# Reordering the front of the expert stage in a two-layer hybrid decoder trunk

## The chip, the cores and the metric

One core of one Trainium2 chip runs the whole kernel. The metric is the device time of one execution in microseconds; three runs of the kernel before are known, and one more execution was profiled.

## The reference, cut to what matters

256 tokens of width 1024 pass two layers. Each layer normalises the tokens with an adaLN modulation (six vectors from `silu(c) @ ada_w`), projects them once, runs three token mixers side by side (retention, a spatial-gating MLP, a sparse attention with three branches), projects back and adds. Then follows a grouped mixture of experts:

```
h2 = rms_norm(x, norm_ffn_g[l]) * (1.0 + sc2) + sh2
probs = softmax(h2 @ router_w); best group of 4, then the top 2 experts in it
for e in range(16):
    a = silu(h2 @ w_gate[e]) * (h2 @ w_up[e])
    out = out + (gates[..., e:e+1] * a) @ w_down[e]
x = x + g2 * out
```

All arrays are float32. The weights of one expert are 4 MB (`w1`, gate and up) and 2 MB (`wd`, down), so the 16 experts of one layer are 96 MB (of 1024 x 1024 bytes), two thirds of what a layer reads.

## The kernel before, in words

The kernel is written with a tile framework. Program order gives each instruction its priority, and a scheduler at build time makes one fixed list for each engine from it: an instruction that is ready by the scheduler's own estimate may go ahead of an earlier one that is not. `tc.issue_after(ins)` forces what is written inside it behind `ins` on the same engine. Buffers are classes with a fixed number: `ring` has 11 slots of 1 MB for all large weights, `wh` 5 buffers of 0.5 MB (the split halves of weights in attention, two quarters of `wd` in the expert stage), `c6` 2 buffers of 1 MB (attention probabilities; the other half of `wd`), `f4` 3 buffers of 0.5 MB (attention operands; the experts' outputs `yy`), `t2` 7 smaller ones. PSUM has 4 banks "W" and 4 banks "D". A DMA on SyncE's queue waits for its buffer, and all behind it wait too.

A layer's attention part splits float32 weights into a rounded part `hi` and a remainder `lo` and multiplies three times (`mm3`). `ORDER[l]` is the order of the loads: `s0` to `s5` are parts of the input projection, `o0` and `o1` the output projection, `a..` the adaLN weights. `S4P` says how many of the eight steps of projection `s4` (retention's gate and the MLP's gate) are written at each of eight places among the four attention heads; what is left comes behind the heads. In the first layer that is all of them, in the second one. `FILL` spreads the adaLN tasks (`ada_half`: two VectorE instructions of 128x1024, L195) over places; two of them stand behind each of the first four experts.

The expert stage (`moe`) computes router and gates on VectorE, ranks tokens per expert with small matmuls (`prank`), and builds the one-hot matrix `Pm` (L1225). `tokens` scales the transposed tokens `xs` by the norm (L887), rounds them to `hi` (L888) on ScalarE and takes `lo = xs - hi` on GpSimd (L890) or VectorE (L892). `gather` multiplies `hi` and `lo` by `Pm` into four PSUM banks and writes `xg`, half by ScalarE (L992), half by VectorE (L990). `group(0)` gathers four fixed experts of full width; then `sort` orders the other twelve by their counts (its result `idI` is read by SyncE's register loads, L1257, to address their weights, and `rkP` by the later gathers). For each expert: one-hot and its transposes (`tables_`, L1025 to L1040), the up-projection into `pgu` (L1049, or L1058 for the experts of small width), activation (L1064), the previous expert's down-projection `py` (L1082) and scatter `mo`. For every expert but a group's first, `LEAD` = 2 of the 8 chunks are multiplied ahead of the tables. `extras` and `overflow` serve experts with more tokens than their width.

Of the kernel before, what the change touches and what calls it, by code (L numbers as in the profile page):

```python
# [23 lines left out]
LEAD = 2  # L24
# [13 lines left out]
F2 = False  # L38
# [7 lines left out]
S4P = ("00000000", "01111111")  # L46
WP = (3, 3)
TASKV = ((2, 3, 4, 5), (2, 3, 4, 5))
XRA = ((1, 1), (1, 0))
# [14 lines left out]
ORDER = ["s3 cmp s5 a01.0 a01.1 a01.2 a01.3 s4 a02.0 a02.1 o1 o0 a02.2 a02.3 a10.0 a10.1 a10.2 a10.3".split(),  # L64
# [778 lines left out]
def moe(tc, nc, l, env):  # L843
# [19 lines left out]
    if True:  # L863
# [18 lines left out]
        def tokens():  # L882
            for q in range(2):
                for tt in range(2):
                    d = slice(512 * q, 512 * q + 512)
                    xs = pts[2 * q + tt]
                    A.activation(xs, xs, AF.Copy, scale=rt[:, tt:tt + 1])  # L887
                    A.copy(hi[:, tt, d], xs)  # L888
                    if XRA[q][tt]:
                        G.tensor_tensor(lo[:, tt, d], xs, hi[:, tt, d].bitcast(F32), op=OP.subtract)  # L890
                    else:
                        late.append(lambda tt=tt, d=d, xs=xs: V.tensor_tensor(lo[:, tt, d], xs, hi[:, tt, d].bitcast(F32), op=OP.subtract))  # L892
# [82 lines left out]
        def gather(Pm, n, xg_):  # L975
            per = 2
            for c0 in range(0, 8, per):
                pg = bank("W", "pgx")
                for u in range(per):
                    k = 0  # L980
                    for tt in range(2):
                        for src in (hi, lo):
                            T.matmul(pg[:, n * u:n * u + n], src[:, tt, P * (c0 + u):P * (c0 + u) + P], Pm[:, tt, :],
                                     start=k == 0, stop=k == 3)
                            k += 1
                for u in range(per):
                    c = c0 + u
                    xg, c_ = xg_(c0, u)
                    if u % 2:
# [224 lines left out]
        def group(g, rank_of):  # L1214
# [8 lines left out]
            for tt in range(2):  # L1223
                for p, o, w, k in runs:
                    V.tensor_tensor(Pm[:, tt, o:o + w * k].rearrange("p (e s) -> p e s", e=k), iot[:, 0:1, 0:w].to_broadcast([P, k, w]),  # L1225
                                    rank_of(tt, p, k).unsqueeze(2).to_broadcast([P, k, w]), op=OP.is_equal)
            xg = []
            while late:
                late.pop(0)()
# [5 lines left out]
            gather(Pm, n, piece)  # L1235
# [7 lines left out]
        last = [None, None, None]  # L1243
        xgs = group(0, lambda tt, p, k: rk[:, tt, ST0 + p:ST0 + p + k])
        rkP, gP, inP, idI, rkx = sort()
        pend, seen, done = None, -1, []
        for g4, members in enumerate(XGR):
            order = members
            for k, (p, xo_, w) in enumerate(order):
# [3 lines left out]
                if p != "x":  # L1253
# [9 lines left out]
                    for i in range(2):  # L1263
                        wb.append(tl("wh", [1024], "wd_"))
                        Y.dma_start(wb[i], sd[:, 1024 * i:1024 * i + 1024])
                    w2_ = tl("c6", [2, 1024], "wd2")
                    Y.dma_start(w2_, sd[:, 2048:4096].rearrange("p (f n) -> p f n", f=2))
                    wb += [w2_[:, 0], w2_[:, 1]]
# [9 lines left out]
                CA = LEAD if k else 0  # L1278
# [10 lines left out]
                if p != "x":  # L1289
                    with fence_(rk_, F2):  # L1290
                        g_["fill"](FILL[l][6][seen])
                if seen == 0:
                    ovf = extras()
# [91 lines left out]
```

## Time and profile before

| | |
|---|---|
| three runs | 864.17, 871.84, 871.11 us; median 871.11 |
| the profiled execution | 865.73 us, of it span 864.1 us |
| TensorE matmul | 762.8 us busy (88%) |
| TensorE weight load | 481.0 us (56%) |
| VectorE | 461.3 us (53%) |
| ScalarE | 278.8 us (32%) |
| GpSimd | 74.7 us (9%) |
| DMA | 292.95 MB, mean 339 GB/s |
| first layer's expert stage | from about 217 to 452 us |
| second layer's expert stage | from about 626 us to the end |

Busy shares are averages over stages with different limits: attention is bound by VectorE and TensorE while loads run ahead, the expert stage by the weights. Matmuls are pipelined, so a busy TensorE is not one at its peak.

### The profile page before, as it was taken

Reading aid. Unit: us, or ns where it says so; the run is one execution under the profiler, and the core shown is the slowest. Engines: PE = TensorE matmul, PEld = TensorE weight load, DVE = VectorE, ACT = ScalarE, POOL = GpSimd, SP = SyncE. Lnnn points to the kernel's source line nnn. Section 1 sums busy time; section 2 is a strip of 40 time slices with the busy share of each in tenths; the row PEclk is TensorE's granted clock in tenths of the full one; section 3 lists DMA queues with packets and bytes.
Section 4 is the critical chain, followed back from the end, with each engine's and each line's share of the span. In section 5 each row is a group of like instructions: output and inputs, shape, how many; then the busy total and the mean of one; then the engine's idle time right before and its main releaser. Section 6 shows DMA issues by size and latency. Waiting matters only on the chain. (4 is left out here: it accounts for less than half of the span.)

```text
span 864.1 us, 14353 instructions
## 1 busy us (share of the span) xinstructions
PE 762.8 (88%) x5460; PEld 481.0 (56%) x5460; DVE 461.3 (53%) x1183; ACT 278.8 (32%) x663; POOL 74.7 (9%) x89
## 2 busy tenths in 40 slices
PE   4789999885899999897988998999789999988795
PEld 3677736784446455343347786678544645534342
DVE  6997869997623223122136898998652322322123
ACT  6246566624111112011026644675411111111010
POOL 2232010211000000000001231011100000000000
PEclk9899869988899999899897998999989999999798
DMA  8959829878779999999999579468838999999995
GB/s 355 420 212 367 334 94 361 293 289 328 279 276 410 418 418 418 417 421 414 420 419 375 178 260 419 149 226 319 300 111 320 421 418 411 419 420 418 414 418 201
DMA packets 46881, 292.95 MB, mean 339 GB/s; under 512 B 5456, under 2 KB 6224, under 8 KB 15952
## 3 DMA queue, kind: packets, MB, share of 16 engines
q1 hardware_dynamic: 45360, 289.76, 84.3%
q10 hardware_dynamic: 1440, 2.16, 0.8%
q8 instruction: 46, 0.75, 0.3%
q14 instruction: 35, 0.29, 0.1%
HBM read 290.84 MB, written 1.05 MB: 338 GB/s over the span
## 5 line engine op out<-in xcount | busy, mean ns | idle before, releaser
L1049 PE MATMUL pgu<-w1slot,xg 128*64 128x512 f32 x640 | 172.5, 627 | 18.3 <-DMA w1slot<-w_dram 13.2
L1049 PEld LDWEIGHTS pgu<-w1slot,xg 128*64 128x64 f32 x640 | 54.9, 141 | 100.4 <-issue 98.8
L195 DVE SCALAR_TENSOR_TENSOR adaslot<-adaslot,sb__90 128x1024 f32<-128x1024 f32 x72 | 92.1, 1290 | 0.0
L1091 DVE SCALAR_TENSOR_TENSOR yy<-py,gc,yy 64x512 fp32r<-64x512 f32 x40 | 30.0, 750 | 112.3 <-ACT yy L1090 112.3
L352 PE MATMUL pz<-hhi,whl 128*128 128x256 f32 x256 | 72.5, 294 | 10.1 <-ACT hhi L423 10.1
L1090 ACT ACTIVATE yy<-py,gc 64x512 fp32r<-64x512 f32 x40 | 27.4, 684 | 165.7 <-PE py L1082 149.5
L353 PE MATMUL pz<-hlo,whl 128*128 128x256 f32 x256 | 74.5, 294 | 0.9 <-DVE hlo L424 0.9
L354 PE MATMUL pz<-hhi,whl 128*128 128x256 f32 x256 | 74.2, 295 | 0.4 <-DVE whl L348 0.2
L348 POOL TENSOR_TENSOR whl<-winslot,whl 128x512 fp32r<-128x512 f32 (+1 forms) x24 | 34.6, 1441 | 388.7 <-ACT whl L346 303.2
L1058 PE MATMUL pgu<-w1slot,xg 128*32 128x256 f32 x896 | 59.6, 387 | 4.0 <-DMA w1slot<-w_dram 4.0
L352 PEld LDWEIGHTS pz<-hhi,whl 128*128 128x128 f32 x256 | 49.2, 197 | 14.1 <-ACT hhi L423 12.9
L1038 DVE CAST pgT<-ppg 128x256 fp32r<-128x256 f32 x34 | 14.4, 424 | 78.2 <-PE ppg L1036 78.2
L1065 DVE TENSOR_TENSOR a<-a,pgu 128x256 f32<-128x256 f32 (+1 forms) x34 | 12.4, 366 | 76.5 <-ACT a L1064 76.3
L353 PEld LDWEIGHTS pz<-hlo,whl 128*128 128x128 f32 x256 | 50.7, 198 | 3.0 <-DVE hlo L424 1.7
L354 PEld LDWEIGHTS pz<-hhi,whl 128*128 128x128 f32 x256 | 50.5, 199 | 2.1 <-DVE whl L348 1.0
L346 ACT CAST whl<-winslot 128x512 fp32r<-128x512 f32 (+1 forms) x72 | 40.5, 578 | 26.2 <-PE pz L354 24.4
L1058 PEld LDWEIGHTS pgu<-w1slot,xg 128*32 128x32 f32 x896 | 28.7, 110 | 33.0 <-issue 16.9
L1064 ACT ACTIVATE a<-pgu 128x256 f32<-128x256 f32 (+1 forms) x34 | 11.6, 341 | 108.4 <-PE pgu L1049 91.7
L348 DVE TENSOR_TENSOR whl<-winslot,whl 128x512 fp32r<-128x512 f32 (+1 forms) x48 | 34.5, 725 | 10.2 <-ACT whl L346 10.0
L1099 ACT ACTIVATE yy<-py,gc 128x256 fp32r<-128x256 f32 x14 | 6.6, 474 | 102.6 <-PE py L1107 102.6
L354 PE MATMUL pw<-yhi,whl 128*128 128x256 f32 x128 | 36.4, 290 | 3.5 <-DVE whl L348 3.5
L1082 PE MATMUL py<-wd,aT 128*64 128x512 f32 x160 | 38.9, 592 | 0.0
(500 smaller groups left out, 1504.7 us busy)
## 6 DMA issues: line engine op xcount, KB each, us to landing
w1slot<-w_dram SPq DMA_DIRECT2D x128, 1024.0 KB, 17.2
adaslot<-adaw_dram SPq DMA_DIRECT2D x40, 1024.0 KB, 6.6
wd<-wd_dram SPq DMA_DIRECT2D x32, 1024.0 KB, 15.1
winslot<-win_dram SPq DMA_DIRECT2D x14, 1024.0 KB, 15.9
slot<-adaw_dram SPq DMA_DIRECT2D x8, 1024.0 KB, 18.9
woslot<-wout_dram SPq DMA_DIRECT2D x8, 1024.0 KB, 11.0
slot<-win_dram SPq DMA_DIRECT2D x6, 1024.0 KB, 18.0
cmpslot<-cmpw_dram SPq DMA_DIRECT2D x4, 1024.0 KB, 13.7
```

The lines of the kernel that those rows point to most:

```text
L195: V.scalar_tensor_tensor(wb, wb, 1.0, sb_, op0=OP.mult, op1=OP.mult, accum_out=mv_[:, b:b + 1])
L346: A.copy(hi, wv)
L348: (G if wc[0] % WP[fl[0]] == 0 else V).tensor_tensor(lo, wv, hi.bitcast(F32), op=OP.subtract)
L352: T.matmul(o, a[0], b[0], start=start, stop=False, skip_group_check=True)
L353: T.matmul(o, a[0], b[1], start=False, stop=False, skip_group_check=True)
L354: T.matmul(o, a[1], b[0], start=False, stop=stop, skip_group_check=True)
L1038: V.tensor_copy(pT, pp_[:, :S])
L1049: lastu[0] = T.matmul(gu[64 * j:64 * j + 64, :], xg(c)[:, xs:xs + CAP], w1(c, j), start=c == 0, stop=c == 7, skip_group_check=True).ins
L1058: lastu[0] = T.matmul(gu[SW * t:SW * t + SW, 0:256], xg(c)[:, xs:xs + SW], wv, start=c == 0, stop=c == 7, skip_group_check=True).ins
L1082: T.matmul(py[64 * hf:64 * hf + 64, :], aT[:, ib, 64 * j:64 * j + 64], wd(fc)[:, 512 * hf:512 * hf + 512], start=fc == 0, stop=fc == 3, sk ...
L1090: ya = A.activation(y[0:64, :], py[r_, :], AF.Copy, scale=gc[r_, :])
L1091: V.scalar_tensor_tensor(y[64:128, :], py[r_, :], gc[r_, :], y[0:64, :].bitcast(F32), op0=OP.mult, op1=OP.subtract)
```

## The change

- `tokens` makes `hi` in one ScalarE instruction from the unscaled `xs`, and all four `lo` in one VectorE instruction each, written behind `Pm`; GpSimd has no part in it.
- `gather` for the first group multiplies all `hi` into four banks, then all `lo`.
- `sort` is written behind the first expert's up-projection and activation, ahead of `extras`; the first expert too multiplies two chunks ahead of its tables.
- The two ada tasks behind the first expert are forced behind `Pm`.
- In the first layer `s4` is loaded behind `a01.0` instead of behind `a01.3`, and seven of its steps stand among the heads.
- The first expert's `wd` is loaded in four pieces, three into `f4` buffers and one into `wh`.

```
-S4P = ("00000000", "01111111")
+S4P = ("01111111", "01111111")
...
-ORDER = ["s3 cmp s5 a01.0 a01.1 a01.2 a01.3 s4 a02.0 a02.1 o1 o0 ...
+ORDER = ["s3 cmp s5 a01.0 s4 a01.1 a01.2 a01.3 a02.0 a02.1 o1 o0 ...
...
-                    A.activation(xs, xs, AF.Copy, scale=rt[:, tt:tt + 1])
-                    A.copy(hi[:, tt, d], xs)
-                    if XRA[q][tt]:
-                        G.tensor_tensor(lo[:, tt, d], xs, hi[:, tt, d].bitcast(F32), op=OP.subtract)
-                    else:
-                        late.append(lambda tt=tt, d=d, xs=xs: V.tensor_tensor(lo[:, tt, d], xs, hi[:, tt, d].bitcast(F32), op=OP.subtract))
+                    A.activation(hi[:, tt, d], xs, AF.Copy, scale=rt[:, tt:tt + 1])
+                    late.append(lambda tt=tt, d=d, xs=xs: V.scalar_tensor_tensor(
+                        lo[:, tt, d], xs, rt[:, tt:tt + 1], hi[:, tt, d].bitcast(F32), op0=OP.mult, op1=OP.subtract))
...
-        def gather(Pm, n, xg_):
+        def gather(Pm, n, xg_, ahead=False):
             per = 2
+            pgs = {}
+
+            def products(c0, srcs):
+                if c0 not in pgs:
+                    pgs[c0] = bank("W", "pgx")
+                for u in range(per):
+                    for src in srcs:
+                        for tt in range(2):
+                            T.matmul(pgs[c0][:, n * u:n * u + n], src[:, tt, P * (c0 + u):P * (c0 + u) + P], Pm[:, tt, :],
+                                     start=src is hi and tt == 0 and u == 0, stop=src is lo and tt == 1, skip_group_check=True)
+            if ahead:
+                for c0 in range(0, 8, per):
+                    products(c0, (hi,))
             for c0 in range(0, 8, per):
...
+                products(c0, (lo,) if ahead else (hi, lo))
...
             xg = []
-            while late:
-                late.pop(0)()
+            with tc.issue_after(pm0[0].ins):
+                while late:
+                    late.pop(0)()
...
-            gather(Pm, n, piece)
+            gather(Pm, n, piece, g == 0)
...
-        rkP, gP, inP, idI, rkx = sort()
...
-                    for i in range(2):
-                        wb.append(tl("wh", [1024], "wd_"))
+                    for i in range(2 if seen else 4):
+                        wb.append(tl("wh" if seen or i == 3 else "f4", [1024], "wd_"))
                         Y.dma_start(wb[i], sd[:, 1024 * i:1024 * i + 1024])
-                    w2_ = tl("c6", [2, 1024], "wd2")
...
+                    if seen:
+                        w2_ = tl("c6", [2, 1024], "wd2")
...
-                CA = LEAD if k else 0
+                CA = LEAD if k or not g4 else 0
...
-                    with fence_(rk_, F2):
+                    with fence_(pm0[0], seen == 0):
                         g_["fill"](FILL[l][6][seen])
                 if seen == 0:
+                    rkP, gP, inP, idI, rkx = sort()
                     ovf = extras()
```

(`F2` was False; `pm0[0]` is the last instruction that builds `Pm`.)

## Rows read from the trace of the kernel before

**Rows 1.** Stretch windows of five stages: busy us, instructions, granted clock, DMA share, GB/s.

```profile
184.00:200.00 16.00, 13.24 (x90) 12.26 (x89) 12.20 (x24) 2.68 (x7) 1.41 (x1) 0.79 0.69 241
...
224.00:248.00 24.00, 22.23 (x94) 8.19 (x96) 9.38 (x44) 2.50 (x4) 0.00 (x0) 0.93 0.46 161
248.00:430.00 182.00, 166.49 (x1300) 84.83 (x1298) 42.19 (x123) 23.42 (x46) 0.00 (x0) 0.95 1.01 417
...
624.00:641.00 17.00, 11.35 (x59) 7.78 (x60) 14.05 (x72) 3.54 (x5) 0.05 (x1) 0.80 0.03 10
...
672.00:848.00 176.00, 163.41 (x1317) 83.26 (x1320) 41.48 (x121) 23.20 (x46) 0.00 (x0) 0.96 1.01 417
```

**Rows 2.** Timeline of SyncE's queue, first layer: start, duration, DMA issues merged.

```profile
198.11 0.33 SPq L1265 DMA_DIRECT2D wd__2228<-wd_dram  x1
...
242.03 0.33 SPq L1265 DMA_DIRECT2D wd__2378<-wd_dram  x1
...
258.41 2.11 SPq L105 DMA_DIRECT2D w1slot<-w_dram  x4
```

**Rows 3.** The same, second layer.

```profile
614.30 0.42 SPq L1265 DMA_DIRECT2D wd__6994<-wd_dram  x1
640.22 5.11 SPq L105 DMA_DIRECT2D w1slot<-w_dram  x4
...
663.62 0.35 SPq L105 DMA_DIRECT2D w1slot<-w_dram  x1
```

**Rows 4.** Waits of SyncE's queue from 605 to 665 us: total, times, longest.

```profile
SPq L1257 <- DVE tmq L1011: 18.5, 1, 18.5
```

**Rows 5.** Timeline of VectorE, first layer, residual update to first expert.

```profile
201.70 1.22 DVE L195 SCALAR_TENSOR_TENSOR adaslot<-adaslot,sb__90 128x1024 f32<-128x1024 f32 x1
...
202.85 0.87 DVE L811 SCALAR_TENSOR_TENSOR xT<-pw,mod,xT 128x256 f32<-128x256 f32 x2
...
207.90 1.21 DVE L195 SCALAR_TENSOR_TENSOR adaslot<-adaslot,sb__90 128x1024 f32<-128x1024 f32 x1
...
211.89 1.17 DVE L926 TENSOR_SCALAR wn<-wn 128x32 f32<-128x32 f32 x1
...
213.06 1.24 DVE L915 TENSOR_TENSOR W<-gsc 128x6 f32<-128x6 f32 x1
214.22 0.15 DVE L916 TENSOR_TENSOR W<-gsc 128x6 f32<-128x6 f32 x1
...
216.92 0.75 DVE L1225 TENSOR_TENSOR Pm<-iot,rk 128x256 fp32r<-128x256 f32 x2
...
218.15 0.68 DVE L892 TENSOR_TENSOR lo<-xs,hi 128x512 fp32r<-128x512 f32 x1
...
225.35 0.47 DVE L1025 TENSOR_SCALAR Pd<-iot,rk 128x128 f32<-128x128 f32 x2
```

**Rows 6.** Timeline of GpSimd, first layer.

```profile
211.76 3.74 POOL L890 TENSOR_TENSOR lo<-xs,hi 128x512 fp32r<-128x512 f32 x3 [6.20 <-ACT hi L888]
```

**Rows 7.** Timeline of TensorE, gather to first up-projection, both layers.

```profile
217.48 0.55 PE L983 MATMUL pgx<-Pm,hi 128*128 128x256 f32 x1 [0.96 <-DVE Pm L1225]
...
225.77 0.30 PE L1034 MATMUL ppg<-ident,Pd 128*128 128x128 f32 x1 [2.99 <-DVE Pd L1025]
...
227.99 10.05 PE L1049 MATMUL pgu<-w1slot,xg 128*64 128x512 f32 x38
...
635.47 0.43 PE L1034 MATMUL ppg<-ident,Pd 128*128 128x128 f32 x2 [3.86 <-DVE Pd L1025]
...
636.17 10.50 PE L1049 MATMUL pgu<-w1slot,xg 128*64 128x512 f32 x40
```

**Rows 8.** Stretch windows of VectorE alone, first layer's heads and behind.

```profile
104.00:128.00 24.00, 14.99 (x49) 0.64 0.35 131
128.00:192.00 64.00, 61.78 (x133) 0.95 0.85 312
```

More of the change, by code (lines that the diff above doesn't have):

```diff
@@ L37 @@
 F1 = True
-F2 = False
 ENG3 = (mybir.EngineType.PE, mybir.EngineType.Activation, mybir.EngineType.DVE, mybir.EngineType.Pool)
@@ L45 @@
 NPA = ("0011", "0011")
-S4P = ("00000000", "01111111")
+S4P = ("01111111", "01111111")
 WP = (3, 3)
 TASKV = ((2, 3, 4, 5), (2, 3, 4, 5))
-XRA = ((1, 1), (1, 0))
 XSV = ((1, 1), (1, 0))
@@ L62 @@
 C3 = TWO_PI - C1 - C2
-ORDER = ["s3 cmp s5 a01.0 a01.1 a01.2 a01.3 s4 a02.0 a02.1 o1 o0 a02.2 a02.3 a10.0 a10.1 a10.2 a10.3".split(),
+ORDER = ["s3 cmp s5 a01.0 s4 a01.1 a01.2 a01.3 a02.0 a02.1 o1 o0 a02.2 a02.3 a10.0 a10.1 a10.2 a10.3".split(),
          "s0 s1 s2 cmp s3 a11.0 a11.1 s5 a11.2 a11.3 s4 a12.0 a12.1 o1 o0 a12.2 a12.3".split()]
@@ L973, in gather_few @@
             return xo
-        def gather(Pm, n, xg_):
+        def gather(Pm, n, xg_, ahead=False):
             per = 2
-            for c0 in range(0, 8, per):
[L978 to L985, printed above, removed]
+            pgs = {}
[10 more added lines that the diff above has]
+                    products(c0, (hi,))
+            for c0 in range(0, 8, per):
+                products(c0, (lo,) if ahead else (hi, lo))
                 for u in range(per):
@@ L988, in gather @@
                     xg, c_ = xg_(c0, u)
+                    pg = pgs[c0]
                     if u % 2:
@@ L1224, in group @@
                 for p, o, w, k in runs:
-                    V.tensor_tensor(Pm[:, tt, o:o + w * k].rearrange("p (e s) -> p e s", e=k), iot[:, 0:1, 0:w].to_broadcast([P, k, w]),
+                    pm0[0] = V.tensor_tensor(Pm[:, tt, o:o + w * k].rearrange("p (e s) -> p e s", e=k), iot[:, 0:1, 0:w].to_broadcast([P, k, w]),
                                     rank_of(tt, p, k).unsqueeze(2).to_broadcast([P, k, w]), op=OP.is_equal)
             xg = []
-            while late:
-                late.pop(0)()
+            with tc.issue_after(pm0[0].ins):
+                while late:
+                    late.pop(0)()
             def piece(c0, u):
@@ L1241, in rank_of @@
             return rkP[:, tt, p:p + k]
-        last = [None, None, None]
+        pm0, last = [None], [None, None, None]
         xgs = group(0, lambda tt, p, k: rk[:, tt, ST0 + p:ST0 + p + k])
-        rkP, gP, inP, idI, rkx = sort()
         pend, seen, done = None, -1, []
@@ L1262, in moe @@
                     wb = []
-                    for i in range(2):
-                        wb.append(tl("wh", [1024], "wd_"))
+                    for i in range(2 if seen else 4):
+                        wb.append(tl("wh" if seen or i == 3 else "f4", [1024], "wd_"))
                         Y.dma_start(wb[i], sd[:, 1024 * i:1024 * i + 1024])
-                    w2_ = tl("c6", [2, 1024], "wd2")
-                    Y.dma_start(w2_, sd[:, 2048:4096].rearrange("p (f n) -> p f n", f=2))
-                    wb += [w2_[:, 0], w2_[:, 1]]
+                    if seen:
+                        w2_ = tl("c6", [2, 1024], "wd2")
+                        Y.dma_start(w2_, sd[:, 2048:4096].rearrange("p (f n) -> p f n", f=2))
+                        wb += [w2_[:, 0], w2_[:, 1]]
                 w1 = lambda c, j, wa=wa: wa[c // 2][:, c % 2, j, :]
```

## The prediction

> **What bounds the kernel now.** I read the stretch windows first. In the expert stage of either layer the DMA engines are full (share 1.01, 417 GB/s) while TensorE is busy 166.5 of 182.0 us and 163.4 of 176.0 us [rows 1]: the weights set the pace there, and TensorE has some 15 and 13 us to spare. What is lost lies in front of it. The DMA share is 0.69 from 184 to 200 us, 0.46 from 224 to 248 us and 0.03 from 624 to 641 us [rows 1]: 5.0, 13.0 and 16.5 us without transfers. Since every later byte follows at full rate, a microsecond of restart gained in these gaps is a microsecond off the end, as long as the restart is what the next expert waits for.
>
> Then SyncE's queue, to see why the DMA stood still. In the first layer the second `wd_` piece of the first expert goes out at 198.11, of the third at 242.03; the fifth expert's first weights at 258.41 [rows 2]. In the second layer SyncE sits after 614.72 for 18.5 us on `tmq`, the sort [rows 3, 4], so until 633.2, spends 7.0 us on the twelve register loads, and issues again at 640.22 [rows 3]. But the ring was full anyway: a slot comes free only when TensorE has done two chunks of the first expert, whose run begins at 636.17 [rows 7]. What holds both restarts is the chain from router to first expert.
>
> That chain is read on VectorE, GpSimd and TensorE together [rows 5 to 7]. The gather starts at 217.48; it ends 2.99 us before 225.77, at 222.78; then TensorE waits for `Pd`, which VectorE reaches only at 225.35, behind the sort. In the second layer the same wait is 3.86 us.
>
> **The change part by part.** Times are of the profiled execution, 865.73 us (span 864.1); the median of the three runs is 871.11, 5.4 us above it, the lowest 1.6 below it.
>
> *One-pass halves.* The three `lo` subtractions on GpSimd span 211.76 to 215.50 [rows 6]. In that span three VectorE instructions of the router take 1.17 to 1.24 us, where their neighbour takes 0.15 [rows 5]: about 1.03 us each, 3.1 us a layer on the path, and they go. Added are four `lo` instructions on VectorE behind `Pm`; the one that is there now takes 0.68 [rows 5], so 2.7 us. The sixteen `hi` products cover them: 32 products take 5.30 us (217.48 to 222.78), half of them 2.65 us, and the first `lo` product needs only two of the four. If that cover were gone, up to 2.7 us would return in each layer. ScalarE issues four instead of eight, and is done before `Pm`.
>
> *Hi products first.* The matmuls are as many as before. They hold all four "W" banks at once, so the first expert's bank waits for the first bank's two evictions, at the end of the gather; I add 0.5 us in the first layer, nothing in the second.
>
> *Sort behind the first expert, two chunks ahead of its tables.* The 2.99 and 3.86 us go: the up-projection needs only `xg`, and the tables come between chunks. What is next late is the gather itself. The sort's VectorE work now runs beside an up-projection of 10.05 and 10.50 us [rows 7]. SyncE's register loads need the sort; the fifth expert's weights are its first user, and they are due some 30 us after the up-projection starts (227.99 to 258.41), so this is covered unless the queue puts them earlier (a rival below).
>
> *The fence.* Two ada tasks, four instructions of 1.22 us (4.9 us) [rows 5], move behind `Pm` in the first layer. The list that the scheduler makes put such instructions in front of the residual update at 201.70 and in front of `lg` and `mx` at 206.47 and 207.90, of which the last is shown [rows 5]. Without the last four the update can go about 0.9 us and `mx` about 1.5 us earlier; I count 2.1. Behind `Pm` they can delay evictions by up to one instruction each; and the two ring slots that they hold are freed some 10 us later, for the third expert, whose weights aren't needed for another 20 us.
>
> *First `wd` in f4.* The output buffers are idle from the end of attention. Two `wh` buffers and half of `c6` come free for the next experts: 1.5 MB more before the restart, and no wait at 198.11 and 242.03. One slot of 1.05 MB takes 2.5 us at 417 GB/s [rows 1]. From 242.03 to 258.41 SyncE issued 7.5 such pieces, 18.9 us of transfer, so the fifth expert's first byte moved only at about 262, 3.6 us behind its issue. With the third expert's `wd` already there, and the fourth's weights drawn from 220 on, this backlog is gone by 250. I count 1.5 of the 3.6 us, since TensorE moves less than that and its finished down-projections still release SyncE. In the second layer there is no such backlog, and I count nothing. The first `wd` goes out as four DMAs of 0.5 MB where three went.
>
> The Trainium skill, DMA: Bandwidth & Descriptors, section Bandwidth, speaks against such a split: it asks for at least 1 MiB in one DMA to get 75% of the peak. By it these 2 MB would take a third longer, an estimate of 1.7 us a layer, and the sum below would be 852.9. The rows speak against it: two of seven DMAs of every expert are 0.5 MB already, and the stage runs at 417 GB/s [rows 1].
>
> *s4 between the heads.* The same instructions in another order, in the first layer alone; its two loads pass six ada loads in SyncE's queue, which then come about 5 us later, long before their tasks. VectorE is busy 61.8 of 64 us from 128 to 192 us, so there the order gives nothing; from 104 to 128 it is busy 15.0 of 24 at a granted clock of 0.64 [rows 8]. Bounds: if that stretch ran at the full 2.4 GHz it would take 24 x 0.64 = 15.4 us, 8.6 us less. If s4's 96 matmuls come into it, at the gather's 0.166 us each, 15.9 us, at most half of that is due to a clock at half rate: 8 us more. The trace shows neither. I take nothing, since VectorE's sum is unchanged and it is the full engine right behind, and keep -8.6 and +8.
>
> *The sum.* First layer: 3.1 + 3.0 + 2.1 - 0.5 = 7.7 us on TensorE, and 1.5 us of backlog: 9.2. Second layer: 3.1 + 3.9 = 7.0. Together 16.2 us: 865.7 - 16.2 = 849.5. A median may lie up to 5.4 us higher, as that of the runs before does; I put it in the middle, 852.
>
> **The rivals.**
>
> *A, VectorE becomes the wait.* Behind `Pm` it now has four `lo`, four evictions, `Pd` and in the first layer four ada instructions. If the queue puts the ada work first, the evictions start 4.9 us later there, and what the `lo` products wait for costs another 1 to 2 us in each layer: the gain is 3 and 5.5 us, with the median 860. For it: the scheduler has put ada work in front of `mx` before [rows 5]. Against: the evictions come earlier in the program.
>
> *B, the sort comes too late for SyncE; slower.* In the second layer SyncE already sat on the sort ahead of expert weights [rows 3, 4]. If the sort is queued behind the first expert's activation, some 11 us after the up-projection's start at about 629, its result is there at about 646 (5 us of sort, as an estimate from half of the time between 216.92 and 225.35 [rows 5], where evictions lie between). Then 7.0 us of loads: the DMA restarts at 653. Seven pieces are missing then, 17.6 us, and the fifth expert's first byte moves at 670 instead of 663.62 [rows 3]: 7 us later. In the first layer, with 4.9 us of ada work in front, it would be 265 instead of 262, 3 us later. With the median 881. It decides from a restart later than 646 in the second layer. Against it: VectorE has the sort's inputs at `Pm`, and time for it.
>
> *C, s4 or the fence spoils attention.* 8 us lost before the router in the first layer; the median is 860. If instead the 8.6 us are gained, 843.
>
> *D, nothing.* The scheduler may give the same order again, or the gap may be refilled by another full buffer (`c6` for the fourth expert is released by the second's down-projection, as before): 866 to 871.
>
> **How the numbers follow.** The sum as it stands has 0.56 (its own range 846 to 857, from the two levels of the runs and the 3.6 us of backlog); A 0.16; C 0.12, a third of it on the fast side; B 0.08; D 0.08. The range that leaves out 2 in 10 goes from 843 to 866: 0.1 lies above (B and part of D), and a tenth below, where C's gain and the whole backlog come together. A measurement of this kernel tells about 1% from no change, 8.7 us, so faster means below 862.4: the forecast, C and most of A, 0.8 with some doubt taken off for terms that share one cause, 0.75; within 1% 0.18; slower 0.07.
>
> **What would show it.** On VectorE no router instruction above 0.3 us between `sel` and `rk`, and GpSimd idle there. TensorE going from the last `lo` product into `pgu` without a wait for `Pd`, at about 218 and 629 us if attention keeps its length. The DMA gap of 224 to 248 down to some 6 us, that of the second layer ending at about 631. SyncE's wait on `tmq` gone, or ending before a ring slot is free. From there the expert stages as long as before, at 417 GB/s. The forecast is wrong if ada instructions stand between `Pm` and the first eviction, if SyncE's loads of the sorted indices end after 646, or if the first layer's attention ends more than 3 us earlier or later, as the start of its router shows.

## The result, and the profile after

| | before | changed |
|---|---|---|
| median of five runs, us | 870.88 (862.22 to 871.84) | 846.35 (842.34 to 856.05) |
| ratio | | 0.973, 95% interval 0.966 to 0.980 |

In the runs of the first experiment the ratio was 0.979 (0.974 to 0.985). The forecast was 852, in the range 843 to 866, and faster. Executions more than 1.5% above their kernel's fastest are disturbed ones, which the ratios leave out and the medians and counts of this document do not; the profiled execution of the five runs (856.05, granted clock 0.66 from 520 to 560 us) is one, so the rows of after come from another execution of the same kernel, 848.38 us with a span of 846.8 (0.74 there): 17.4 us below the profiled execution of before.

The stretch windows of the changed kernel, beside [rows 1]:

```profile
184.00:200.00 16.00, 13.61 (x109) 12.77 (x107) 13.69 (x25) 4.10 (x10) 3.58 (x2) 0.89 0.88 310
...
216.00:240.00 24.00, 22.72 (x116) 11.53 (x117) 19.18 (x73) 4.13 (x7) 0.00 (x0) 0.92 0.82 318
240.00:430.00 190.00, 177.45 (x1366) 88.01 (x1366) 45.69 (x129) 26.14 (x50) 0.00 (x0) 0.95 1.01 414
604.00:624.00 20.00, 18.55 (x123) 11.53 (x123) 15.60 (x62) 8.67 (x20) 0.00 (x0) 1.00 0.67 245
655.00:831.00 176.00, 162.88 (x1321) 82.94 (x1324) 41.49 (x121) 23.46 (x46) 0.00 (x0) 0.96 1.01 411
```

The gap of 13.0 us in the first layer is now 24 x (1 - 0.82) = 4.3 us, and the one of 16.5 us in the second is 20 x (1 - 0.67) = 6.6. The expert stages behind them run as before, DMA full, TensorE not.

SyncE's queue, the timeline of the first layer and then of the second (start, duration, issues merged):

```profile
207.33 18.71 SPq L103 DMA_DIRECT2D w1slot<-w_dram  x4
...
226.57 0.56 SPq L1267 DMA_DIRECT2D wd__2376<-wd_dram  x1
...
251.33 1.94 SPq L103 DMA_DIRECT2D w1slot<-w_dram  x4
...
621.55 8.06 SPq L103 DMA_DIRECT2D w1slot<-w_dram  x6
```

And its longest wait from 590 to 650 us (total, times, longest):

```profile
SPq L103 <- PE ppg L1036: 14.1, 1, 14.1
```

The third expert's second `wd_` piece goes out at 226.57 where it went at 242.03 [rows 2]; the fifth expert's first weights at 251.33, not 258.41. In the second layer SyncE issues again at 621.55, not 640.22 [rows 3]; its wait for the sort [rows 4] is gone, and it waits for a free ring slot instead.

VectorE in the first layer, beside [rows 5]:

```profile
209.03 0.19 DVE L893 TENSOR_REDUCE mx<-lg 128x2 f32<-128x32 f32 x1
...
211.89 0.17 DVE L921 TENSOR_SCALAR wn<-wn 128x32 f32<-128x32 f32 x1
...
212.04 0.16 DVE L910 TENSOR_TENSOR W<-gsc 128x6 f32<-128x6 f32 x1
...
213.79 0.75 DVE L1227 TENSOR_TENSOR Pm<-iot,rk 128x256 fp32r<-128x256 f32 x2
214.47 2.73 DVE L886 SCALAR_TENSOR_TENSOR lo<-xs,rt,hi 128x512 fp32r<-128x512 f32 x4
217.12 0.47 DVE L1027 TENSOR_SCALAR Pd<-iot,rk 128x128 f32<-128x128 f32 x2
219.60 0.55 DVE L992 TENSOR_SCALAR xg<-pgx,gs,mod 128x256 f32<-128x256 f32 x1 [2.01 <-ACT xg L994]
...
221.85 1.21 DVE L193 SCALAR_TENSOR_TENSOR adaslot<-adaslot,sb__90 128x1024 f32<-128x1024 f32 x1
...
230.35 0.16 DVE L1017 CAST idI<-inP 128x12 int32<-128x12 f32 x1
```

No router instruction above 0.3 us is left (`wn` 0.17, `W` 0.16, where 1.17 and 1.24 stood), `Pd` is done before the gather ends, and the ada instructions come behind the evictions. That is what the prediction asked to see of VectorE.

TensorE, beside [rows 7]:

```profile
214.36 3.75 PE L980 MATMUL pgx<-Pm,hi 128*128 128x256 f32 x16 [1.01 <-DVE Pm L1227]
217.91 2.85 PE L980 MATMUL pgx<-Pm,lo 128*128 128x256 f32 x16
220.68 1.94 PE L1051 MATMUL pgu<-w1slot,xg 128*64 128x512 f32 x8
...
223.26 12.24 PE L1051 MATMUL pgu<-w1slot,xg 128*64 128x512 f32 x56
...
237.77 1.08 PE L1084 MATMUL py<-wd__2185,aT 128*64 128x512 f32 x4 [0.96 <-issue]
...
614.31 0.17 PE L936 MATMUL prank<-o,ub 128*128 128x16 bf16 x1 [0.44 <-DVE o L924]
...
615.59 2.14 PE L980 MATMUL pgx<-Pm,hi 128*128 128x256 f32 x16 [1.01 <-DVE Pm L1227]
617.57 2.08 PE L980 MATMUL pgx<-Pm,lo 128*128 128x256 f32 x16
619.58 1.94 PE L1051 MATMUL pgu<-w1slot,xg 128*64 128x512 f32 x8
```

In both layers TensorE goes from the last `lo` product into `pgu` with no wait, at 220.68 and 619.58 us. The prediction named 218 and 629: in the first layer the router started 0.9 us later than before and the chain behind it gave less than forecast, and for the second layer it had not taken off what the first layer saves. Two things here were not in the prediction. The second layer's gather takes 4.0 us, at a granted clock of 1.00 (2.4 GHz). And 64 up-projection matmuls stand ahead of the first `py`: an expert has 32 (one expert's run between two down-projections), so the second expert's whole up-projection now precedes the first expert's down-projection. That first `py` comes 237.77 - 220.68 = 17.1 us behind the first `pgu`, where before it was 240.95 - 226.00 = 15.0.

### A measure for the experiments

The same kernel's runs lie over some 16 us, and much of that is in attention, which of these edits only s4 and the fence touch. So beside the ratios I read three rows of each trace: the last router matmul of either layer (`pl<-sel,lq`) and the end of the first layer's last `py`. Of the changed kernel:

```profile
207.50 0.59 PE L835 MATMUL pl<-sel,lq 128*128 128x16 f32 x4
...
440.02 1.05 PE L1109 MATMUL py<-wd,aT 128*32 128x256 f32 x16
...
608.74 0.59 PE L835 MATMUL pl<-sel,lq 128*128 128x16 f32 x4
```

Of the kernel before:

```profile
206.56 0.59 PE L837 MATMUL pl<-sel,lq 128*128 128x16 f32 x4 [0.95 <-DVE rt L869]
...
448.86 1.05 PE L1107 MATMUL py<-wd,aT 128*32 128x256 f32 x16
...
616.05 0.59 PE L837 MATMUL pl<-sel,lq 128*128 128x16 f32 x4
```

First layer: 441.07 - 207.50 = 233.6 us from router to end, 243.4 before. Second layer, to the end of the span: 846.8 - 608.74 = 238.1, 248.1 before. "Sum" below is the two together, "attention" the stretch between them. The profiled execution of the five runs gives 473.8 as its sum (232.5 and 241.4), this one 471.6 (233.6 and 238.1): 1.1 us of repeat in the first layer and 3.3 in the second, and a difference between two kernels below that shows nothing.

A shorter stretch repeats better. From the last router matmul to the first `pgu` the two executions take 13.19 and 13.18 us in the first layer and 10.84 and 10.84 in the second; this stretch is called the chain below. What spreads lies behind it. From the first `pgu` to the end the second layer takes 226.6 to 230.8 us in all fourteen traces, in no order by edit (before: 227.9). The first layer takes 219.0 to 220.6 in the eleven traces that have the `wd` prefetch, 223.9 before.

| kernel | median us (runs) | ratio to before, interval | router 1 | layer 1 | attention | layer 2 | sum |
|---|---|---|---|---|---|---|---|
| before | 866 to 869 (59) | 1 | 206.6 | 243.4 | 166.1 | 248.1 | 491.4 |
| e1_after, changed | 847.4 (6) | 0.979, 0.974 to 0.985 | 207.5 | 233.6 | 167.7 | 238.1 | 471.6 |
| e2_s4 | 845.3 (6) | 0.978, 0.973 to 0.983 | 206.1 | 232.8 | 167.2 | 241.6 | 474.4 |
| e3_wd | 856.1 (13) | 0.991, 0.987 to 0.994 | 214.3 | 241.2 | 174.8 | 241.1 | 482.4 |
| e4_sort | 869.2 (12) | 1.006, 1.002 to 1.010 | 207.7 | 244.2 | 166.5 | 249.0 | 493.2 |
| e5_tok | 856.6 (10) | 0.990, 0.985 to 0.995 | 207.5 | 237.0 | 162.3 | 243.6 | 480.6 |
| e6_fence | 850.8 (10) | 0.978, 0.973 to 0.984 | 209.2 | 231.3 | 168.6 | 237.4 | 468.7 |
| e7_best | 837.6 (4) | 0.970, 0.960 to 0.980 | 199.8 | 230.0 | 162.3 | 239.5 | 469.4 |
| e8_front | 848.8 (1) | | 204.9 | 238.8 | 164.4 | 239.1 | 478.0 |
| e9_best5 | 849.5 (6) | 0.974, 0.967 to 0.982 | 206.2 | 229.8 | 174.1 | 241.5 | 471.3 |
| e10_warm | 849.8 (6) | 0.983, 0.977 to 0.989 | 209.4 | 230.6 | 163.8 | 239.6 | 470.2 |
| e11_ahead | 857.3 (4) | 0.990, 0.981 to 0.998 | 207.6 | 232.7 | 175.5 | 239.6 | 472.4 |
| e12_sortfence | 870.0 (10) | 1.002, 0.996 to 1.008 | 208.1 | 239.0 | 175.3 | 246.9 | 485.9 |

### The profile page after: what moved, and what is told of

It reads as the page before. It is cut to its first block, busy times and chain, and to the rows that moved or that the text cites. A ratio compares the mean times of both kernels' runs of the same rounds, so it can differ in the third digit from the quotient of the medians.

```text
span 854.5 us, 14344 instructions
## 1 busy us (share of the span) xinstructions
PE 762.8 (89%) x5460; PEld 480.2 (56%) x5460; DVE 459.3 (54%) x1189; ACT 273.4 (32%) x655; POOL 68.0 (8%) x83
## 5 line engine op out<-in xcount | busy, mean ns | idle before, releaser
L1051 PE MATMUL pgu<-w1slot,xg 128*64 128x512 f32 x640 | 168.5, 623 | 18.3 <-PEq L1188 9.8
L1051 PEld LDWEIGHTS pgu<-w1slot,xg 128*64 128x64 f32 x640 | 51.7, 141 | 101.0 <-issue 97.9
L193 DVE SCALAR_TENSOR_TENSOR adaslot<-adaslot,sb__90 128x1024 f32<-128x1024 f32 x72 | 94.5, 1324 | 0.0
L350 PE MATMUL pz<-hhi,whl 128*128 128x256 f32 x256 | 75.0, 304 | 10.2 <-ACT hhi L421 10.2
L352 PE MATMUL pz<-hhi,whl 128*128 128x256 f32 x256 | 76.3, 304 | 0.5 <-DVE whl L346 0.4
L350 PEld LDWEIGHTS pz<-hhi,whl 128*128 128x128 f32 x256 | 51.1, 205 | 14.4 <-ACT hhi L421 13.1
L351 PEld LDWEIGHTS pz<-hlo,whl 128*128 128x128 f32 x256 | 52.5, 205 | 3.0 <-DVE hlo L422 1.7
L352 PEld LDWEIGHTS pz<-hhi,whl 128*128 128x128 f32 x256 | 51.9, 204 | 3.6 <-issue 2.1
L1060 PEld LDWEIGHTS pgu<-w1slot,xg 128*32 128x32 f32 x896 | 28.6, 109 | 33.8 <-issue 16.5
L350 PE MATMUL pw<-yhi,whl 128*128 128x256 f32 x128 | 37.6, 295 | 5.5 <-DVE mod L194 3.9
L352 PE MATMUL pw<-yhi,whl 128*128 128x256 f32 x128 | 36.9, 295 | 2.3 <-DVE whl L346 2.2
## 6 DMA issues: line engine op xcount, KB each, us to landing
w1slot<-w_dram SPq DMA_DIRECT2D x128, 1024.0 KB, 16.2
wd<-wd_dram SPq DMA_DIRECT2D x30, 1024.0 KB, 14.7
```

Of the source, the lines that this page charges most:

```text
L193: V.scalar_tensor_tensor(wb, wb, 1.0, sb_, op0=OP.mult, op1=OP.mult, accum_out=mv_[:, b:b + 1])
L350: T.matmul(o, a[0], b[0], start=start, stop=False, skip_group_check=True)
L351: T.matmul(o, a[0], b[1], start=False, stop=False, skip_group_check=True)
L352: T.matmul(o, a[1], b[0], start=False, stop=stop, skip_group_check=True)
L1051: lastu[0] = T.matmul(gu[64 * j:64 * j + 64, :], xg(c)[:, xs:xs + CAP], w1(c, j), start=c == 0, stop=c == 7, skip_group_check=True).ins
L1060: lastu[0] = T.matmul(gu[SW * t:SW * t + SW, 0:256], xg(c)[:, xs:xs + SW], wv, start=c == 0, stop=c == 7, skip_group_check=True).ins
```

## The experiments

**e1_after: the changed kernel again.** No edit.

> The changed kernel once more, as the mark for the three kernels beside it, and for a profile at the clock that the kernel before had. My theory: 846 us (842 to 850), 0.973 of the kernel before; from the second layer's last router matmul to its first up-projection about 9.7 us where 19.0 were, in the first layer about 12, the fifth expert's first weights at about 252 where 258.4 were. If the gain were a matter of the clock in attention, the profile would show attention in the first layer to be shorter than before, with the router starting ahead of 207.6 us; by my theory it starts within 3 us of it.

From the last router matmul to the first `pgu` it takes 619.58 - 608.74 = 10.8 us in the second layer (20.1 before) and 13.2 in the first (19.4 before); the expectation counted from `lg`, some 1 us behind. The router starts 0.9 us later than before, not earlier: the gain lies behind the routers, 19.8 us of sum, and not in attention. Of these the chains give 6.3 and 9.3 us; 3.5 lie behind the first layer's chain, and 0.7, within repeat, behind the second's.

**e2_s4: s4 of the first layer in its old place.**

```diff
-S4P = ("01111111", "01111111")
+S4P = ("00000000", "01111111")
-ORDER = ["s3 cmp s5 a01.0 s4 a01.1 a01.2 a01.3 a02.0 ...
+ORDER = ["s3 cmp s5 a01.0 a01.1 a01.2 a01.3 s4 a02.0 ...
```

> The change without its s4 part: s4 of the first layer stands behind the heads again, on its old engine pattern. My theory (s4 costs and gives nothing): within 3 us of the changed kernel, 846. Rival: the 7 us by which the change gave more than the 16.2 of my sum come from attention in the first layer; then this kernel takes 853, and its router starts about 7 us later. If s4 spoils attention, it is 2 to 8 us faster than the changed kernel: 838 to 844.

The ratios of the two kernels lie 0.001 apart, well inside either interval. The rival that s4 gave the excess over my sum falls. In the traces the router of the first layer starts at 206.1 with s4 in its old place and at 207.5 with it between the heads; the other traces agree as to sign (old place: 199.8 to 206.6 in five traces; new: 207.5 to 214.3 in nine), but no time shows it.

**e3_wd and e8_front: the first wd as before,** with s4 as changed and with s4 as before.

```diff
-                    for i in range(2 if seen else 4):
-                        wb.append(tl("wh" if seen or i == 3 else "f4", [1024], "wd_"))
+                    for i in range(2):
+                        wb.append(tl("wh", [1024], "wd_"))
...
-                    if seen:
-                        w2_ = tl("c6", [2, 1024], "wd2")
...
+                    w2_ = tl("c6", [2, 1024], "wd2")
...
```

> The change with the first expert's wd loaded as before, in three DMAs into wh and c6. My theory: the first layer's restart is again held by DMA backlog, so 1.5 to 3.6 us of the gain go there, and nothing in the second layer: 848 to 850, and the third expert's wd goes out behind the first expert's down-projection, at about 240 us where it was 227. Rival: without the free buffers the shorter chain is worth nothing in the first layer, since the transfers are late anyway: 854 to 856. If the prefetch is hidden: 846.

> The change without its s4 and wd parts: one-pass halves, hi products first, the sort behind the first expert, the fence. It is to show where the 10 us went that the kernel without the wd part lost. My theory: the second wd piece of the third expert has to wait for the first expert's down-projection, which now stands behind the second expert's whole up-projection, some 17 us behind the first up-projection's start, and SyncE's queue stands behind it: the DMA has a gap of 6 to 8 us there (240 to 248 us), and the expert stage of the first layer is that much longer: 852 to 857. Rival: the loss lies ahead of the router (the wd loads wait longer for buffers there and the attention of the first layer ends later); then the router starts 5 us later or more, and there is no such gap.

The ratio rises by 0.0114, 9.9 us on the 866.4 of before: beyond the 1.5 to 3.6 us of my theory, by the size of the rival. In e3_wd's trace the router also starts late (214.3), in that of e8_front it does not (204.9, against e2_s4's 206.1), so the place is read from e8_front. One window of its first layer:

```profile
232.00:240.00 8.00, 6.70 (x36) 2.85 (x32) 3.81 (x17) 1.06 (x2) 0.00 (x0) 1.00 0.28 78
```

And its SyncE queue:

```profile
223.25 0.42 SPq L1267 DMA_DIRECT2D wd__2372<-wd_dram  x1
236.05 0.33 SPq L1267 DMA_DIRECT2D wd__2374<-wd_dram  x1
```

The second piece of the third expert's `wd` waits from 223.7 to 236.05 for the first expert's down-projection, which starts at 234.94 there, 17.1 us behind the first `pgu`. The fourth expert's weights are queued behind it, and the DMA stands still for 8 x 0.72 = 5.8 us. That is the length of the loss: layer 1 takes 238.8 us against e2_s4's 232.8, 6.0 more (e3_wd against e1_after: 7.6). Layer 2 is 2.5 us shorter in the one pair and 3.0 longer in the other, both within its repeat. The rival that the loss lies ahead of the router falls for e8_front, and as a reason for the 7.6 us in e3_wd too: there the first expert's weights already go out 6.3 us later than in e1_after (186.32 against 179.99) and its first `wd` piece only behind them, at 199.10, so the late router was there before any `wd` load. The time of e8_front does not show the loss: it is one execution, its 848.8 us lie below the 852 to 857 expected, and e2_s4's profiled one took 849.4; a shorter attention (2.8 us), an earlier router (1.2) and the second layer (2.5) hide it.

Part of the prefetch's worth does not hang on the sort's move. Before, too, the third expert's second piece waits for the first down-projection, until 242.03 [rows 2], and e4_sort and e12_sortfence below, with the prefetch and the sort in its old place, take 220.3 and 220.5 us from the first `pgu` to the layer's end, where before took 223.9 (no clean pair: their other edits, ahead of that stretch, differ from before as well). With the sort moved the pairs are 219.9 against 225.9 and 220.4 against 227.8. So the prefetch is worth some 3.5 us beside the old place and 6.0 to 7.4 beside the new one, where the first `py` comes later.

**e4_sort and e12_sortfence: the sort in front again,** with that expert's tables ahead of its up-projection; e12 with the fence off as well.

```diff
         xgs = group(0, lambda tt, p, k: rk[:, tt, ST0 + p:ST0 + p + k])
+        rkP, gP, inP, idI, rkx = sort()
...
-                CA = LEAD if k or not g4 else 0
+                CA = LEAD if k else 0
...
                 if seen == 0:
-                    rkP, gP, inP, idI, rkx = sort()
                     ovf = extras()
```

> The change with the sort in front of the first expert and that expert's tables ahead of its whole up-projection, as before; the one-pass halves, the hi products first, the fence, s4 and wd as changed. My theory: TensorE waits for the tables again, 3.0 us in the first layer and 3.9 in the second, a little longer since the lo instructions stand in front: 853 to 855, and a wait for Pd ahead of the first up-projection in both layers. Rival: the expert stages have slack enough, and the gain is in the router and the gather: 846 to 848. Second rival: with the reordering gone too, which now puts the second expert's up-projection ahead of the first's down-projection, it costs more than the waits: 857 or more.

It takes the whole gain away, some 15 us beyond my 853 to 855: the second rival's number, though hardly by its reason. The chains take 23.80 and 20.38 us, where the changed kernel's take 13.18 and 10.84: 20.2 of the 21.6 us of sum lie ahead of the first `pgu`, and little is left for the order of projections behind it. TensorE's waits in both layers:

```profile
230.23 0.66 PE L1036 MATMUL ppg<-ident,Pd 128*128 128x128 f32 x2 [9.34 <-DVE Pd L1027]
...
637.50 0.66 PE L1036 MATMUL ppg<-ident,Pd 128*128 128x128 f32 x2 [8.25 <-DVE Pd L1027]
638.74 3.68 PE L1051 MATMUL pgu<-w1slot,xg 128*64 128x512 f32 x8
```

VectorE in the first layer, the first of three ada instructions and then `Pd`:

```profile
222.39 1.22 DVE L193 SCALAR_TENSOR_TENSOR adaslot<-adaslot,sb__90 128x1024 f32<-128x1024 f32 x1
...
229.81 0.47 DVE L1027 TENSOR_SCALAR Pd<-iot,rk 128x128 f32<-128x128 f32 x2
```

The waits are 9.34 and 8.25 us where before they were 2.99 and 3.86: the `lo` instructions (2.7 us) now stand in front of the sort, the ada instructions that the fence released stand inside it, and behind the wait the first eight matmuls run at half rate (3.68 us against 1.94, at a granted clock of 0.50).

> The change with the sort in front of the first expert and its tables ahead, as before, and with the fence off; halves, hi products first, s4 and wd as changed. With the fence on, this took 869: TensorE waited 9.34 and 8.25 us for Pd, since VectorE had the lo instructions, the evictions, the sort and three and two ada instructions of 1.22 us in front of it. My theory: without the ada instructions there, the waits fall to about 5.7 and 5.8 us and the kernel to 860 to 863, so that the price of the old place of the sort is some 15 us beside the other parts, where the trace of before showed 3.0 and 3.9. Rival: the waits stay at 8 to 9 us because other work fills the place, and the time stays at 866 to 869.

Rows of TensorE in e12:

```profile
225.33 0.66 PE L1036 MATMUL ppg<-ident,Pd 128*128 128x128 f32 x2 [4.83 <-DVE Pd L1027]
...
639.43 0.66 PE L1036 MATMUL ppg<-ident,Pd 128*128 128x128 f32 x2 [6.14 <-DVE Pd L1027]
```

The waits fell to 4.83 and 6.14, close to what my theory said, and the sum by 7.3 us against e4. The ratio fell by only 0.0045, and the two intervals leave room for nothing and for 0.012 (10 us); the time was 870, where I expected 860 to 863 and the rival 866 to 869. The waits bear the theory out, the time does not. Against e6_fence, with the fence off in both, the sort's old place costs 17.2 us of sum, of which 13.6 lie in the chains (18.49 and 18.29 against 12.31 and 10.84): not 3.0 and 3.9. My reading is that the cover that made it cheap before (a slower router chain and gather, with the sort done beside them) is gone; no run puts the cover back alone.

**e5_tok: the token halves as before,** two passes on ScalarE, three subtractions on GpSimd.

```diff
-                    A.activation(hi[:, tt, d], xs, AF.Copy, scale=rt[:, tt:tt + 1])
-                    late.append(lambda ...: V.scalar_tensor_tensor(lo[:, tt, d], xs, rt[:, tt:tt + 1], hi[:, tt, d] ...))
+                    A.activation(xs, xs, AF.Copy, scale=rt[:, tt:tt + 1])
+                    A.copy(hi[:, tt, d], xs)
+                    if ((1, 1), (1, 0))[q][tt]:
+                        G.tensor_tensor(lo[:, tt, d], xs, hi[:, tt, d].bitcast(F32), op=OP.subtract)
+                    else:
+                        late.append(lambda ...: V.tensor_tensor(lo[:, tt, d], xs, hi[:, tt, d] ...))
```

> The change with the token halves made as before: ScalarE in two passes, three of the four lo subtractions on GpSimd and one on VectorE; hi products first, the sort behind the first expert, fence, s4 and wd as changed. My theory: three router VectorE instructions take about 1.2 us again, 3.1 us in each layer on the chain, and TensorE starts the gather 3 us later behind the last router matmul (10 us where it is 6.9); in the second layer the longer idle time brings the half clock back into the gather, another 1.6 us. 6 to 8 us slower than the changed kernel: 853 to 855. Rival: VectorE's four lo instructions cost as much as the stalls, since Pd and the evictions stand behind them: then 846 to 848, with the gather's end no later.

GpSimd in the first layer:

```profile
211.79 3.73 POOL L888 TENSOR_TENSOR lo<-xs,hi 128x512 fp32r<-128x512 f32 x3 [4.59 <-ACT hi L886]
```

VectorE there:

```profile
211.93 1.17 DVE L924 TENSOR_SCALAR wn<-wn 128x32 f32<-128x32 f32 x1
...
213.09 1.24 DVE L913 TENSOR_TENSOR W<-gsc 128x6 f32<-128x6 f32 x1
```

TensorE in the second layer:

```profile
615.53 0.17 PE L939 MATMUL prank<-o,ub 128*128 128x16 bf16 x1 [3.59 <-DVE o L927]
...
616.82 3.75 PE L983 MATMUL pgx<-Pm,hi 128*128 128x256 f32 x16 [1.01 <-DVE Pm L1230]
620.37 2.96 PE L983 MATMUL pgx<-Pm,lo 128*128 128x256 f32 x16
```

The long instructions are back at once, in the same places. From the last router matmul to the gather it takes 10.0 us in both layers, against 6.86 and 6.85: 3.1 to 3.2 us a layer. And in the second layer TensorE is idle 3.59 us ahead of the rank matmuls instead of 0.44, and the gather takes 6.44 us instead of 3.99. The ratio is 0.011 above the changed kernel's, 9.4 us, a little more than the 6 to 8 expected; the sum is 9.0 above, 8.8 of it in the chains. The Trainium skill, SBUF — State Buffer, section Who interferes with whom, says that a VectorE instruction with two SBUF inputs contends with a GpSimd instruction that reads SBUF, and that whoever comes second is blocked until the other is done. For `W`, a TENSOR_TENSOR, the trace agrees: the stalled one takes 1.24 us, as long as one of GpSimd's subtractions (3.73 / 3). The stalled `wn` (1.17 us) is a TENSOR_SCALAR with one tensor input, which that sentence does not cover.

**e6_fence: the fence off.**

```diff
-                    with fence_(pm0[0], seen == 0):
+                    with fence_(pm0[0], False):
```

> The change without the fence: the two ada tasks of the first layer may again be listed ahead of the router. My theory by the sum: up to 2.1 us slower, 846 to 849, with ada instructions ahead of the residual update and of mx. Rival from the profile after: behind Pm these four instructions of 1.22 us stand in front of the sort and of the first expert's activation, and the first down-projection comes 17.1 us behind the up-projection's start where it was 15.0; without them there it comes some 2 us earlier, and the kernel is 0 to 3 us faster: 843 to 846.

No difference in the ratio. In the trace ada instructions of VectorE start at 204.34, 206.34 and 209.03, the last in front of `lg`, and the router starts 1.7 us later (209.2 against 207.5); behind the routers the sum is 2.9 us shorter, 2.3 of it in the first layer, of which a shorter gather gives 0.8 (5.49 against 6.32) and an earlier first `py` 0.4. Both my step and the rival point the right way, and neither is shown: the changed kernel's other execution has its router at 208.3 and 232.5 us in the first layer, 0.9 and 1.2 from this one.

**e11_ahead: hi and lo in turn.**

```diff
-            gather(Pm, n, piece, g == 0)
+            gather(Pm, n, piece, False)
```

> The change with the gather's products in the old order, hi and lo in turn, bank by bank. My theory: the four lo instructions on VectorE (2.73 us, behind Pm) are no longer covered, since the second product needs the first lo; the two lo halves come 0.7 us apart, and the first bank's products wait 1 to 2 us, the later ones not: 1 to 2 us in each layer less what the earlier evictions give back: 847 to 850. In the second layer, whose gather takes 4.0 us, the full 2.7 us can show: up to 4 us in all. If the order is worth nothing: 846.

The gather takes 6.27 us against 6.32 in the first layer, and 4.39 against 3.99 in the second: 0.4 us for both. The list still puts eight `hi` products first in either layer, and the `lo` halves mostly come as fast as the products ask for them. The four runs (857.3, 0.990) lie above the 847 to 850 expected and 9.9 us above the changed kernel's; their interval of 0.017 overlaps its interval, and the trace has 7.8 us of it in attention (175.5 against 167.7), ahead of which this edit touches only the first layer's gather. The sum is 0.8 longer. The order of the products is worth nothing that these rows show beyond 0.4 us.

**e10_warm, e7_best, e9_best5: 24 warm-up matmuls in the first layer's router,** as the second layer has; e7 and e9 (the same kernel) with s4 back in its old place too.

```diff
-WARM = (1, 6)
+WARM = (6, 6)
```

> The change with s4 of the first layer in its old place and 24 warm-up matmuls instead of 4 in the first layer's router, as the second layer has. In the changed kernel the first layer's gather takes 6.3 us, its first sixteen products 3.75 where the second layer's take 2.14. If it is the idle TensorE ahead of it that sets this, the gather takes about 4.0 us here too, and the kernel is 2 us faster than with s4 undone alone: 843. If the warm-ups stand in the way of the rank matmuls, these come later than 5.6 us behind the last router matmul, and the time is 846 to 849. As a version to keep it would be 842 to 844.

> The version with s4 undone and 24 warm-ups once more, in more rounds, since the first four runs spread over 14 us. By the chain it is 2 us shorter in the first layer than with s4 undone alone (gather 4.0 us where 5.95 were), and nothing else: 0.975 of the kernel before. The first look gave 0.970 with a granted clock of 0.961 in the profiled run; if the warm-ups also keep the clock up elsewhere, the ratio stays at 0.970 or below, and the clock of its runs lies above those of the changed kernel (0.923 to 0.944).

> The change as it is, with 24 warm-ups in the first layer alone. If the warm-ups give the 2 us of the gather: 0.977 of the kernel before, where the changed kernel had 0.979. If s4 between the heads costs 1.4 us, as the start of the router says (207.5 against 206.1), it stays 1 to 2 us above the version with s4 undone.

TensorE of e10 in the first layer:

```profile
214.99 0.17 PE L936 MATMUL prank<-o,ub 128*128 128x16 bf16 x1 [0.45 <-DVE o L924]
...
216.27 2.15 PE L980 MATMUL pgx<-Pm,hi 128*128 128x256 f32 x16 [1.01 <-DVE Pm L1227]
```

The gather takes 4.0 us here too (216.27 to the first `pgu` at 220.27), and layer 1 is 3 us shorter than without (230.6 against 233.6; 229.8 and 230.0 against 232.8 with s4 back), 2.0 to 2.7 of it in the chain. The times don't confirm it: 0.970 and 0.974 in two sets of the same kernel, 0.983 for e10. The first set's median, 837.6, was not met again. Nor do the warm-ups keep the clock up elsewhere: the runs of e9 have mean clocks of 0.927 to 0.960, those of the changed kernel 0.923 to 0.949, and only e9's fastest run lies above them. A version that beats the changed kernel is likely by the trace and not shown by the times.

## Why the prediction was right

**The place was right.** The chain from router to first expert held both restarts. It is 6.3 and 9.3 us shorter, the DMA gaps closed as described, and the stages behind kept their pace. The sum said 16.2 us for the profiled execution; the profiled executions differ by 17.4, the medians by 24.5, the ratios by 18 to 24. The granted clock is part of that spread: through 152 runs (each kernel with its own level, one slope for all) the time falls by 6.1 us for 0.01 of mean granted clock, with a scatter of 2.2, and at 0.935 the kernel before takes 865.0 and the changed one 849.3, 15.7 us less. Through the 113 of them that the ratios rest on it is 4.9 us for 0.01, and 16.8 us less. Part of the difference in clock may be the change's own work (the second layer's gather runs at 1.00, where before it ran at 0.56 in its first 3.6 us), so these are lower views of the gain, and the ratios stand.

**That 16.2 lies so near 17.4 is in part luck.** The sum put 14.7 us into the two chains and they give 15.5, but 6.3 for the 7.7 of the first and 9.3 for the 7.0 of the second; the 1.5 us of backlog became 3.5; and a router that starts 0.9 us later and an attention 1.6 us longer, neither of them in the sum, took 2.5 back.

**One-pass halves, 3.1 us a layer: right, and too small in the second.** The stalls are 3.1 us in either (e5). But the shorter idle time there also lifts the gather to the full clock, 2.4 us more in that pair and 1.6 against before, which I did not count.

**The Pd waits, 3.0 and 3.9 us: gone as said.** Of the chain's 6.1 us behind the second layer's gather start, 3.86 are that wait, 1.6 the faster gather (5.6 to 4.0), and 0.7 the tables that now come between chunks. In the first layer, 2.2 us: the gather itself is 1 us longer, at a granted clock of 0.50 for its first 3.5 us and 0.69 behind, where before it was 0.50 for 2.7 us and 0.98 behind. The 0.5 us for the first bank's evictions did not show: `pgu` follows the last `lo` product directly. Nor did the 1.7 us a layer show that the rule of the Trainium skill (DMA: Bandwidth & Descriptors, section Bandwidth) would take for DMAs of 0.5 MB: the layer that loads its first `wd` in four of them is 6.0 to 7.6 us shorter than with three, and the stage behind runs at 414 GB/s; a smaller cost inside that net gain was not tried. What the step missed is that its price depends on the other parts: put back alone, it costs 13.6 and 20.2 us in the chains (e12, e4).

**The backlog, 1.5 us for the first wd: the term that was mis-sized.** The step took the first down-projection to stay where it was relative to the up-projection. The new list puts it 2.1 us later, behind the second expert's whole up-projection, and so a `wd` in the old buffers would hold SyncE until then. The prefetch is worth 6.0 and 7.6 us of the first layer in two pairs, 5.8 to 7.2 by the two fits on the clock and about 10 by the ratio; beside the sort's move it is not a small extra, since without it that layer gains 4.6 and 2.2 us instead of 10.6 and 9.8. Net, from the first `pgu` to the last `py` of the layer it is 220.4 us, 223.9 before: 3.5, where I counted 1.5, at the upper bound of 3.6. The two kernels with the sort in its old place come to 220.3 and 220.5 as well, so the 3.5 us do not hang on the sort's move, and what erred was the step from 3.6 to 1.5.

**The fence, 2.1 us: 0.9 of it seen.** From the router to the gather the first layer lost 4.06 us and the second 3.16, and the 0.9 between them fits the ada instruction that stood between `lg` and `mx`. The rest was to be an earlier router, which starts 0.9 us later than before. In e6, without the fence, it starts 1.7 us later still; I costed the four instructions behind `Pm` at nothing, and they may take about as much back, both within repeat.

**s4, nothing: held** within what the times can tell, with a router start some 1.4 us later, on the slow side of the bounds. **Hi products first: cover hardly needed.** Without it the gather is 0.4 us longer in the second layer and no longer in the first, whose products start at half rate (e11).

**The rivals.** A fell as stated: the evictions come ahead of the ada instructions, although VectorE is busy 7.9 of the 8 us from 224 to 232, and the late first `py` may be its echo. That it is VectorE's load and not only the list that puts it there was argued, not shown: with the fence off it still comes 16.7 us behind. B fell: `idI` is there at 230.35 in the first layer and at 628.59 in the second, 9.0 us behind the first `pgu`, and SyncE's second-layer issues resume at 621.55. C and D fell.

## What to carry to other kernels

When several edits shorten one chain, cost each with the others in place: the sort's old place cost 6.9 us of waits before and 13.6 to 20.2 us beside the other edits, and the prefetch some 3.5 us with the sort in front and 6.0 to 7.4 behind, where a down-projection comes later. Ask of each moved step which buffer release moves with it, and what the DMA queue holds behind that buffer. Where runs spread over 2% in a stretch that the change leaves alone, measure from a landmark behind that stretch, take the shortest stretch that holds the effect, and quote the repeat of that measure.

## What was not expected of the hardware

- TensorE's clock on a short chain. After a wait of 3.6 us and a few small matmuls, sixteen products of 128x256 took 3.75 us, at a granted clock of 0.50 (1.2 GHz); after a wait of 0.44 us, 2.14 us at 1.00 (2.4 GHz) (e5_tok against e1_after, second layer; e1_after against e10_warm, first). Some 2.3 us hang on what stands in front of the gather, not on the gather.
- Attention in the second layer has the same instructions in all kernels here, and took from 162.3 to 175.5 us. In one stretch of it the granted clock was 0.83 in e5_tok (162.3 us), 0.59 in e1_after (167.7) and 0.50 in e9_best5 (174.1); the windows of the three in that order:

```profile
520.00:540.00 20.00, 17.05 (x85) 11.64 (x86) 16.73 (x48) 15.22 (x59) 2.60 (x2) 0.83 0.70 294
```

```profile
520.00:540.00 20.00, 20.00 (x75) 12.39 (x73) 12.88 (x39) 12.99 (x51) 1.63 (x2) 0.59 0.53 220
```

```profile
520.00:540.00 20.00, 20.00 (x67) 12.99 (x67) 9.62 (x32) 12.08 (x47) 1.27 (x1) 0.50 0.45 187
```

The three programs stand up to 8.5 us apart there; counted from the end of the first layer, in the 20 us that are 520 to 540 in e1_after, the clocks are 0.83, 0.59 and 0.57, and in the 10 us behind 1.00, 0.80 and 0.50. What sets the clock there was not tried. The spread of 13 us is more than the effect of most edits in this study.
